# One more Strassen pair in the input projection of a hybrid layer, with bank pools in turn, other queue positions for right operands, and an approximate root with one Newton step

## The chip, the cores and the metric

The kernel runs on one core of a Trainium2 chip. The metric is device time in microseconds (us), of which the median of several runs is given. The engines are named as in the profile: PE (TensorE, matmuls; PEld its weight loads), DVE (VectorE), ACT (ScalarE), POOL (GpSimd), SP (SyncE, which issues the DMAs). SBUF is the memory of 128 partitions, PSUM holds eight banks of 128x512 float32 into which PE accumulates.

## The reference

One layer over 1024 positions of width 1024, in float32:

```python
u = rms_norm(x, norm1_g)
z = u @ w_in                      # 1024 x 3584: conv B, C, h; retention q, k, v, gate
y_conv = group_rms_norm(cb * causal_dwconv3(cc * ch, conv_w), conv_norm_g, 8)
q, k = rotary(rq), rotary(rk) * 128 ** -0.5
o = chunkwise_retention(q, k, v)  # 4 heads of 128, chunks of 128, per-head decay
y_ret = group_rms_norm(o, ret_norm_g, 4) * silu(rg)
x = x + concat(y_conv, y_ret) @ w_out
x = x + relu(rms_norm(x, norm2_g) @ w_up) ** 2 @ w_down
out = rms_norm(x, final_norm_g)
```

## The kernel before, in words

All data lies transposed: features on the partitions, the 1024 positions along the free axis in two halves of 512. So a matmul has a 128x128 block of weights as its left operand and 128x512 of data as its right, and sums into one bank. For accuracy each operand is split into a high part (`wh`, `uh`, `yh`, a cast on ACT) and the rest (`wl`, `ul`, `yl`, a subtraction on DVE or POOL), and each block product is three matmuls: high·high, high·rest, rest·high (`mm`, whose matmuls stand at line 375).

The input projection has 24 tiles f of 128 columns, plus v. A **whole** tile (`tile_in`) takes 8 blocks of rows and two halves of positions: 48 matmuls of 128x512. A **pair** of tiles (`pair_in`) is one Strassen-Winograd step over two column tiles, two halves of the rows and two halves of the positions: seven products, each over four blocks of 128 rows, 12 matmuls each. The left operands of the products are sums of weight blocks that `Left.split` makes on POOL; the right operands are quarters of x ("11", "21", "22") and four sums of them, t1 to t4. `rights(j)` makes these for the four row blocks j: it loads x again (`xs`), scales it on ACT, subtracts on DVE or POOL, casts the high part on ACT (`put_hi`, tile `U`) and subtracts for the rest (`put_lo`). Only t1, which product n=5 needs, is written over the second half of `uh[0..3]` and `ul[0..3]`, so it has to wait until the last whole tile has read these. The results of products are added into the two z tiles on DVE.

The order in time is: v; q and k of heads 0, 1 and then 2, 3 (whole tiles 12 to 19, with the retention as a background task that puts a few small matmuls between them); the whole tiles `IN_WHOLE[0]`, then the list `IN_WHOLE[1]`; the pairs `IN_PAIRS`; the output projection in four groups of two tiles; the MLP, also in Strassen products. Tiles 0 to 11 are the conv group (for conv block i, f = 3i is C, 3i+1 h, 3i+2 B), 12 to 19 retention's q and k, 20 to 23 its gates.

A tile's evacuation starts background tasks: `conv_h` (the product with h and the convolution of three taps), `conv_b` (the product with B, then the group norm) and `gate`. The norm of a conv block (`norm`) squares y on ACT, splits the squares, sums them over groups of 64 partitions with two matmuls against `blkr` (lines 455 and 456), takes the square root on ACT and the reciprocal on DVE, and multiplies y by it.

What stands where in each engine's queue is set by a planner at build time: `background` holds an estimated clock for each engine, with a cost per column (`Engine`), and `now` advances by `SLOT` per 12 matmuls. An operation is handed out when its estimated start is less than `LOOK` ahead of `now`, and, where it may go to DVE or POOL, to the one that would end first; matmuls of background tasks come when the task has been ready for `PE_MARGIN`. The queues themselves are served strictly in order. All operations of ACT, DVE and POOL go through the wrapper `Engine`, so that the profile has them at line 65; line 375 is `mm`, 554 to 621 the retention, 1195 the MLP's second product. Banks come from two pools of four, `pm` and `pr`.

Of the kernel before, what the change touches and what calls it, by code (L numbers as in the profile page):

```python
# [16 lines left out]
P = 128  # L17
# [17 lines left out]

IN_WHOLE = [[0, 1, 2], [3, 4, 5, 6, 7]]
IN_PAIRS = [(8, 9), (10, 11), (20, 21), (22, 23)]
IN_FIRST = [12, 13, 16, 17, 14, 15, 18, 19] + IN_WHOLE[0] + IN_WHOLE[1]  # L40
SLOT, LOOK, PE_MARGIN, LATE = 2.57, 2.0, 1.2, 0.0
UP_ORDER, MLP_ORDER = (1, 2, 5, 6, 3, 7, 4), (1, 2, 6, 5, 3, 7, 4)
IN_LAST = (1, 5, 2, 6, 7, 4, 3)


class Engine:


    def __init__(self, engine, per_column, now, clock):
        self.engine, self.per_column, self.now, self.clock = engine, per_column, now, clock  # L50
        clock[self] = 0.0

    def cost(self, n, op=""):
        return 1e-3 * n * (6.4 if op == "reciprocal" else self.per_column)

    def __getattr__(self, op):
        f = getattr(self.engine, op)

        def call(out, *args, **kw):
            n = 1  # L60
            for d in out.shape[1:]:
                n *= d
            begin = max(self.clock[self], self.now[0])
            self.clock[self] = begin + self.cost(n, op)
            return f(out, *args, **kw)  # L65

        return call
# [3 lines left out]
def hybrid_layer(  # L71
# [14 lines left out]
):  # L86
    nc = tc.nc
    now, clock, procs, got = [0.0], {}, [], {}
    act = Engine(nc.scalar, 1.02, now, clock)
    dve = Engine(nc.vector, 1.18, now, clock)  # L90
    pool = Engine(nc.gpsimd, 2.4, now, clock)
    gammas = [1.0 - 2.0 ** (-5.0 - h) for h in range(NH)]

    cp = ctx.enter_context(tc.tile_pool(name="cp", bufs=1))
# [81 lines left out]

    IN_ORDER = IN_FIRST + [f for pair in IN_PAIRS for f in pair]
    blocks = [w_in[f, c] for f in IN_ORDER for c in range(2)]
    blocks += [w_out[i, c] for j in range(4) for i in (j, 4 + j) for c in range(2)]
    mix = Stream(rw, blocks, 3)  # L180

    def next_piece():
# [4 lines left out]
    class Left:  # L187


        def __init__(self, stream, n_, order=UP_ORDER):  # L190
            self.stream, self.n = stream, n_
            self.five_first = 5 in order[:2]
            self.raw = None
# [36 lines left out]
    dve.memset(blk[64:128, 64:128], 1.0)  # L230
    blkr = xp.tile([P, P], F32R, name="blkr")
    dve.tensor_copy(blkr, blk)
    ident = cp.tile([P, P], F32, name="ident")
    make_identity(nc, ident)

# [164 lines left out]
    def background(look=LOOK):  # L400
        while True:
            best = None
            for task in list(procs):
                want = task.want
                if want is None:
                    if task.ready + PE_MARGIN <= now[0] or look > 1e6:
# [36 lines left out]
    def norm(y, w, inv_n, done):  # L443
# [11 lines left out]
        nc.tensor.matmul(b, w, sh, start=True, stop=False)  # L455
        nc.tensor.matmul(b, w, slo, start=False, stop=True)
        now[0] += 0.43
        parts_of_s[0] -= 1
# [6 lines left out]
        parts_of_s[0] -= 1  # L465

    def norms():
        while asked and parts_of_s[0] <= 2:
# [41 lines left out]
    def rot_tiles(ct, st):  # L510
# [21 lines left out]

        tile_in(evac)
        return q

    o_n, retention_task = {}, [None, None]

    def retention(p, q, k):
# [7 lines left out]
        for c in range(NC_ + 2):  # L546
# [28 lines left out]
            if done is not None:  # L575
# [83 lines left out]
    def conv_b(i, half, z, out, psum):  # L659
# [6 lines left out]
        eng.tensor_mul(o, o, cvs[i][:, sl])  # L666
        y[i] = out

        def done(rt):
# [42 lines left out]
    for p in range(2):  # L712
# [79 lines left out]
    def pair_in(fs, last):  # L792
# [3 lines left out]
        for at, n in enumerate(order):  # L796
            if not got.get("pairs") and n in (6, 7, 4):
                for j in range(4):
                    force(({6: "t2", 7: "t3", 4: "t4"}[n], j))
            b = product(n, pm)  # L800
            slot()
            prepare()
            ready = None
# [9 lines left out]
            if n == 6:  # L813
                dve.tensor_add(c12, acc, b5)
            if n == 7:
                dve.tensor_add(c22, acc, b5)
                ready = 1, 1
            if n == 3:
                dve.tensor_add(c12, c12, b)
                ready = 0, 1  # L820
            if n == 4:
                ready = 1, 0
# [622 lines left out]
```

## Time and profile before

| | |
|---|---|
| median of 3 runs | 1099.43 us (1099.06 to 1100.08) |
| the profiled execution, its time | 1098.8 us |
| its span in the trace | 1097.0 us |
| mean granted clock of PE | 0.986 of full speed |
| retention's last matmuls end | 208.4 us from the span's start |
| first matmul of the output projection | 366.49 us |

The stages up to 208 us are v, q, k and most of the retention with the whole tiles around it; 208 to 366 us hold the rest of the whole tiles and the four pairs; the output projection lasts to some 470 us, the MLP to the end. In the views a group shows the operation, "out<-in", its shape and count, then busy time and the mean of one; a wait shows the engine and line that waited and what released it.

### The profile page before, as it was taken

What the parts mean: (1) busy time and instruction counts of PE and PEld (TensorE: products, weight loads), DVE (VectorE), ACT (ScalarE), POOL (GpSimd) and SP (SyncE); (2) the same over time, 40 slices, a digit from 0 to 9 for tenths busy, and PEclk for the clock granted to TensorE, in tenths of its full rate; (3) what the DMA queues carried; (4) which work ended last, traced back from release to release, by engine and by line L of the source; (5) the groups of instructions that cost most, each with busy time, mean ns of one, the idle gap of its engine ahead of it and who ended that gap; (6) DMA issues with size and microseconds to landing.
All of it is one profiled execution on the core that took longest, in us unless ns stands there. A gap on an engine that the chain in (4) does not pass through costs nothing.

```text
span 1097.0 us, 13933 instructions
## 1 busy us (share of the span) xinstructions
PE 1064.2 (97%) x4916; PEld 885.6 (81%) x4916; DVE 874.1 (80%) x1206; ACT 461.6 (42%) x909; POOL 544.7 (50%) x377
## 2 busy tenths in 40 slices
PE   8999999998999899989999999999999999999997
PEld 6888888886777688878888888888888888888886
DVE  8446534597999756589999989989999899899945
ACT  8211344663435444435343433443443443334453
POOL 6133312264667213537729538358267185384553
PEclk9999999999999899989999999999999999999998
DMA  7111110510111525040130121211201301200204
GB/s 269 61 58 48 30 39 30 183 39 20 49 58 49 191 97 189 3 164 20 48 97 27 46 82 39 70 47 48 87 29 50 96 20 48 87 20 20 76 3 154
DMA packets 38869, 76.49 MB, mean 70 GB/s; under 512 B 4368, under 2 KB 6544, under 8 KB 38800
## 3 DMA queue, kind: packets, MB, share of 16 engines
q1 hardware_dynamic: 38800, 75.61, 21.2%
q8 instruction: 39, 0.64, 0.2%
q14 instruction: 30, 0.25, 0.1%
HBM read 68.78 MB, written 6.82 MB: 69 GB/s over the span
## 4 chain that ended last, share of the span: by engine, by line
PE 84%; DVE 10%; ACT 3%; issue 2%; POOL 1%; DMA 0%; SPq 0%; DVEq 0%; POOLq 0%; ACTq 0%
PE b L375 54%; PE b L1195 24%; PE b L331 2%; DVE wl L65 2%; DVE U L65 1%; DVE z L65 1%; ACT uh L65 1%; ACT t L65 1%; DVE cv L65 1%; DVE r L65 1%; DVE t L65 1%; PE b L583 1%; PE b L554 1%; DVE q L65 1%; PE b L312 1%
## 5 line engine op out<-in xcount | busy, mean ns | idle before, releaser
L65 ACT CAST wh<-r 128x512 fp32r<-128x512 f32 x286 | 177.2, 621 | 373.4 <-PE b L375 183.9
L65 DVE TENSOR_TENSOR wl<-r,wh 128x512 fp32r<-128x512 f32 x253 | 230.0, 912 | 106.5 <-ACT wh L65 105.8
L375 PE MATMUL b<-U,wh 128*128 128x512 f32 x992 | 308.1, 392 | 2.9 <-DVE U L65 2.9
L65 POOL TENSOR_TENSOR r<-r,r 128x512 f32<-128x512 f32 x136 | 208.2, 1533 | 126.5 <-DVE wl L65 77.5
L1195 PE MATMUL b<-V,wh 128*128 128x512 f32 x784 | 242.0, 389 | 0.4 <-POOL V L65 0.4
L375 PEld LDWEIGHTS b<-U,wh 128*128 128x128 f32 x992 | 187.5, 189 | 42.6 <-DVE U L65 3.4
L65 DVE TENSOR_TENSOR x<-x,b 128x512 f32<-128x512 f32 (+1 forms) x320 | 197.9, 663 | 26.5 <-PE b L375 25.8
L375 PE MATMUL b<-U,wl 128*128 128x512 f32 x496 | 194.2, 392 | 0.0
L1195 PEld LDWEIGHTS b<-V,wh 128*128 128x128 f32 x784 | 147.1, 188 | 31.8 <-POOL V L65 0.8
L65 POOL TENSOR_TENSOR t<-t,t 128x512 f32<-128x512 f32 x70 | 106.7, 1529 | 102.3 <-ACT t L65 56.0
L1195 PE MATMUL b<-V,wl 128*128 128x512 f32 x392 | 152.5, 389 | 0.0
L65 POOL TENSOR_TENSOR wl<-r,wh 128x512 fp32r<-128x512 f32 x33 | 44.2, 1341 | 150.7 <-ACT wh L65 126.2
L375 PE MATMUL b<-uh,wh 128*128 128x512 f32 x320 | 107.7, 401 | 4.0 <-DVE z L65 4.0
L375 PEld LDWEIGHTS b<-U,wl 128*128 128x128 f32 x496 | 93.8, 189 | 19.5
L375 PE MATMUL b<-ul,wh 128*128 128x512 f32 x320 | 106.0, 396 | 0.0
L375 PE MATMUL b<-uh,wl 128*128 128x512 f32 x320 | 105.6, 395 | 0.0
L1195 PEld LDWEIGHTS b<-V,wl 128*128 128x128 f32 x392 | 73.6, 188 | 15.2
L65 POOL TENSOR_TENSOR V<-t,V 128x512 fp32r<-128x512 f32 x35 | 48.7, 1393 | 68.4 <-ACT V L65 68.4
L65 DVE TENSOR_TENSOR t<-t,b 128x512 f32<-128x512 f32 x112 | 75.8, 677 | 1.7 <-POOL t L65 1.2
L375 PEld LDWEIGHTS b<-uh,wh 128*128 128x128 f32 x320 | 59.8, 192 | 16.4 <-issue 2.7
L375 PEld LDWEIGHTS b<-uh,wl 128*128 128x128 f32 x320 | 61.2, 191 | 13.3
L375 PEld LDWEIGHTS b<-ul,wh 128*128 128x128 f32 x320 | 60.9, 190 | 13.1
(158 smaller groups left out, 1424.7 us busy)
## 6 DMA issues: line engine op xcount, KB each, us to landing
r<-w_up_t SPq DMA_DIRECT2D x64, 256.0 KB, 2.6
r<-w_down_t SPq DMA_DIRECT2D x56, 256.0 KB, 2.6
r<-w_in_t SPq DMA_DIRECT2D x48, 256.0 KB, 2.6
xt<-xT SPq DMA_DIRECT2D x16, 256.0 KB, 5.4
xs<-xT SPq DMA_DIRECT2D x8, 512.0 KB, 7.3
r<-w_out_t SPq DMA_DIRECT2D x16, 256.0 KB, 2.6
x<-xT SPq DMA_DIRECT2D x8, 512.0 KB, 7.7
outT<-out SPq DMA_DIRECT2D x6, 512.0 KB, 2.9
```

What stands on the lines that cost most here:

```text
L65: return f(out, *args, **kw)
L312: nc.tensor.matmul(b[:, c * P : (c + 1) * P], d, ident, start=True, stop=True)
L331: nc.tensor.matmul(vb[i], a[k][:, tsl], b[k // 2][:, vs], start=(k == 0 and a is uh and b is vh), stop=(k == KT - 1 and a is ul),)
L375: nc.tensor.matmul(b, a[:, k, :], rhs(n, k)[r], start=(start and i == 0), stop=(stop and i == len(ops) - 1),)
L554: nc.tensor.matmul(bs[:, js[j]], k[j][:, sl], q[j][:, sl], start=True, stop=True)
L583: nc.tensor.matmul(bo[:, js[j]], sc[:, js[j]], vj[j], start=True, stop=(S is None))
L1195: nc.tensor.matmul(b, a, r, start=(i == 0), stop=(i == len(ops) - 1))
```

## The change

Tiles 6 and 7 leave the list of whole tiles and become the first of five pairs. The seven products of a pair take their banks from `pm` and `pr` in turn, and the last pair's order puts n=5 sixth, whose bank is then added to both z tiles where it was held until n=6 and n=7. `spread_norms` and the first three whole tiles come after the tasks `rights` are created, so that their queue positions can lie among conv and retention. The norm takes ACT's approximate reciprocal root `r`, and a square of it scaled by half the group's factor; DVE then multiplies that by the bank's sum (plus eps), which gives half of (mean + eps)·r², multiplies y by r and −g, and by (that − 1.5): one Newton step, y·g·r·(1.5 − ½(mean + eps)·r²). The retention's root on 128x2 gets a Newton step in the same way. `NORM_MARGIN` is the time that a norm's squares must have been ready before its matmuls are placed. The planner's costs become a fixed part and a part per column, with more for a DVE operation without a bank beside a busy POOL. In the output projection, the four steps of a group change their order, and with them the order of the weight blocks.

```diff
-IN_WHOLE = [[0, 1, 2], [3, 4, 5, 6, 7]]
-IN_PAIRS = [(8, 9), (10, 11), (20, 21), (22, 23)]
+IN_WHOLE = [[0, 1, 2], [3, 4, 5]]
+IN_PAIRS = [(6, 7), (8, 9), (10, 11), (20, 21), (22, 23)]
...
-SLOT, LOOK, PE_MARGIN, LATE = 2.57, 2.0, 1.2, 0.0
+SLOT, LOOK, PE_MARGIN, LATE = 2.72, 2.0, 1.2, 0.0
+NORM_MARGIN = 4.0
...
-IN_LAST = (1, 5, 2, 6, 7, 4, 3)
+IN_LAST = (1, 2, 6, 7, 4, 5, 3)
...
-    def cost(self, n, op=""):
-        return 1e-3 * n * (6.4 if op == "reciprocal" else self.per_column)
+    def cost(self, n, op="", bank=False):
+        per_column = 6.3 if op == "reciprocal" else self.per_column
+        cost = self.fixed + 1e-3 * n * per_column
+        if self.beside and not bank and op != "reciprocal":
+            begin = max(self.clock[self], self.now[0])
+            cost += min(cost, max(0.0, 0.6 * (self.clock[self.beside] - begin)))
+        return cost
...
-    act = Engine(nc.scalar, 1.02, now, clock)
-    dve = Engine(nc.vector, 1.18, now, clock)
-    pool = Engine(nc.gpsimd, 2.4, now, clock)
+    act = Engine(nc.scalar, 0.13, 0.95, now, clock)
+    pool = Engine(nc.gpsimd, 0.2, 2.5, now, clock)
+    dve = Engine(nc.vector, 0.13, 1.04, now, clock, pool)
...
-    blocks += [w_out[i, c] for j in range(4) for i in (j, 4 + j) for c in range(2)]
+    blocks += [w_out[i, c] for j in range(4) for c in range(2) for i in (j, 4 + j)]
...
-            part = split_piece({1: a11, 2: a12, 3: a12, 4: a22, 5: a21, 6: a11, 7: a21}[n])
+            s3 = a11 if self.seven_first else a21
+            part = split_piece({1: a11, 2: a12, 3: a12, 4: a22, 5: a21, 6: a11, 7: s3}[n])
...
-            if n == (2 if self.five_first else 5):
-                pool.tensor_sub(a21, a22, a11)
+            if n == (6 if self.seven_first else 2 if self.five_first else 5):
+                pool.tensor_sub(s3, a22, a11)
...
-        yield None
+        yield NORM_MARGIN
...
-        act.activation(rt, b, AF.Sqrt, bias=eps, scale=inv_n)
+        less = xp.tile([P, H], F32, tag="s", name=nm("r"), bufs=4)
+        act.activation(rt, b, AF.Abs_reciprocal_sqrt, bias=eps, scale=inv_n)
+        act.activation(less, rt, AF.Square, scale=(0.5 * inv_n) ** 0.5)
         yield (dve,)
-        dve.reciprocal(rt, rt)
-        yield from done(rt)
...
+        dve.scalar_tensor_tensor(less, b, EPS / inv_n, less, ALU.add, ALU.mult)
+        yield from done(rt, less)
...
-            dve.scalar_tensor_tensor(o, o, sm[:, CG + i : CG + i + 1], rt, ALU.mult, ALU.mult)
+            dve.scalar_tensor_tensor(o, o, less_g[:, i : i + 1], rt, ALU.mult, ALU.mult)
+            dve.scalar_tensor_tensor(o, less, 1.5, o, ALU.subtract, ALU.mult)
...
-                act.activation(m, m, AF.Sqrt)
-                dve.reciprocal(m, m)
+                m = rsqrt(m, xp.tile([P, 2, 2], F32, tag="m2", name=nm("m"), bufs=4))
...
-    spread_norms(rows_)
-    for f in IN_WHOLE[0]:
-        whole(f)
-
...
+    spread_norms(rows_)
+    for f in IN_WHOLE[0]:
+        whole(f)
     for f in IN_WHOLE[1]:
...
-            b = product(n, pm)
+            b = product(n, (pm, pr)[at % 2])
...
-            if n == 5:
-                b5 = b
...
+            if last:
+                if n == 6:
+                    act.copy(c12, acc)
+                if n == 7:
+                    act.copy(c22, acc)
+                if n == 5:
+                    dve.tensor_add(c22, c22, b)
+                    dve.tensor_add(c12, c12, b)
+                    ready = 1, 1
+            else:
+                if n == 5:
+                    b5 = b
+                if n == 6:
+                    dve.tensor_add(c12, acc, b5)
+                if n == 7:
+                    dve.tensor_add(c22, acc, b5)
+                    ready = 1, 1
...
-        steps = [(a, 0, 0), (a, 1, 0), (b, 0, 0), (b, 1, 0), (a, 0, 1), (b, 0, 1), (a, 1, 1), (b, 1, 1)]
+        steps = [(a, 0, 0), (b, 0, 0), (a, 1, 0), (b, 1, 0), (a, 0, 1), (b, 0, 1), (a, 1, 1), (b, 1, 1)]
```

Three places show what the planner makes of it. A row has the line, the operation, what is written, what is read, and the shape; the numbers behind the names tell tiles apart.

The first is ACT's queue ahead of the four casts `uh<-xs` of t1, on which product n=5 of the first pair rests. Before, where the last whole tiles run:

```order
L65 COPY a_2273<-b_2193 128x512
L65 COPY a_2273<-b_2194 128x512
L65 ACTIVATE r_2280<-b_2276,eps 128x512
L65 CAST wh_2309<-r_2180 128x512
L65 CAST wh_2339<-r_2077 128x512
L65 ACTIVATE cv_2348<-a_2273,sm 128x512
L65 CAST uh_142<-xs_1895 128x512
L65 CAST uh_143<-xs_1913 128x512
L65 CAST uh_144<-xs_1917 128x512
L65 CAST uh_145<-xs_1921 128x512
L65 CAST wh_2374<-r_2130 128x512
L65 COPY z_2360<-b_2361 128x512
```

After, from the last scaling of x for these transforms:

```order
L73 ACTIVATE xs_2120<-xs_2120,sm 128x1024
L73 CAST U_2220<-xs_2112 128x512
L73 CAST U_2227<-xs_2116 128x512
L73 CAST U_2231<-xs_2115 128x512
L73 CAST U_2235<-xs_2116 128x512
L73 CAST U_2238<-xs_2120 128x512
L73 CAST U_2242<-xs_2119 128x512
L73 CAST U_2245<-xs_2120 128x512
L73 CAST uh_144<-xs_1365 128x512
L73 CAST uh_145<-xs_2111 128x512
L73 CAST uh_146<-xs_2115 128x512
L73 CAST uh_147<-xs_2119 128x512
```

Before, the casts of t1 stand among weight casts (`wh`) and conv work of the whole tiles, far behind the casts of `U`; now they stand directly behind the last scaling, the casts of `U` for t2 to t4, and nothing else.

DVE's queue at the same place after the change, from the end of the last whole tile (its banks `b_2124` and `b_2125` are read by the first two rows) on, is next:

```order
L73 TENSOR_TENSOR z_2206<-b_2124,R 128x512
L73 TENSOR_TENSOR z_2206<-b_2125,R 128x512
L73 TENSOR_TENSOR U_2209<-xs_2112,U_2209 128x512
L73 TENSOR_TENSOR z_2206<-z_2206,cv_2138 128x512
L73 TENSOR_TENSOR U_2214<-xs_2111,U_2214 128x512
L73 TENSOR_TENSOR z_2206<-z_2206,cv_2138 128x512
```

```order
L73 TENSOR_TENSOR U_2235<-xs_2116,U_2235 128x512
L73 TENSOR_TENSOR U_2238<-xs_2120,U_2238 128x512
L73 TENSOR_TENSOR U_2242<-xs_2119,U_2242 128x512
L73 TENSOR_TENSOR U_2245<-xs_2120,U_2245 128x512
L73 TENSOR_TENSOR ul_152<-xs_1365,uh_144 128x512
L73 TENSOR_TENSOR ul_153<-xs_2111,uh_145 128x512
L73 TENSOR_TENSOR ul_154<-xs_2115,uh_146 128x512
L73 TENSOR_TENSOR ul_155<-xs_2119,uh_147 128x512
L73 TENSOR_TENSOR z_2256<-z_2257,b_2282 128x512
```

Between these two pieces stand eight rows of the same kinds: the `U` of the other parts and the differences `xs`. The four rows `ul` are the rest parts of t1, and the row behind them is the first addition of a product into z.

The second place is the norm on DVE, among the pairs. Before, at a gate's tile (`z_2690`) and the norm of conv block 2's y (`z_2528`):

```order
L65 TENSOR_TENSOR z_2689<-z_2690,b_2744 128x512
L65 RECIPROCAL r_2793<-r_2793 128x512
L65 TENSOR_TENSOR z_2689<-z_2689,b_2798 128x512
L65 TENSOR_TENSOR z_2690<-z_2690,b_2816 128x512
L65 TENSOR_TENSOR z_2690<-z_2690,b_2744 128x512
L65 SCALAR_TENSOR_TENSOR z_2528<-z_2528,sm,r_2793 128x512
L65 RECIPROCAL r_2795<-r_2795 128x512
L65 TENSOR_TENSOR wl_2854<-r_2684,wh_2853 128x512
L65 TENSOR_TENSOR z_2690<-z_2690,b_2840 128x512
L65 SCALAR_TENSOR_TENSOR z_2528<-z_2528,sm,r_2795 128x512
```

After, at a gate's tile (`z_2936`, `z_2937`) and the norm of the last conv block's first half (`z_2577`):

```order
L73 SCALAR_TENSOR_TENSOR o_834<-z_2751,sm,o_834 128x512
L73 SCALAR_TENSOR_TENSOR r_2932<-b_2928,r_2932 128x512
L73 TENSOR_TENSOR wl_2978<-r_2795,wh_2977 128x512
L73 TENSOR_TENSOR z_2936<-z_2937,b_2964 128x512
L73 SCALAR_TENSOR_TENSOR z_2577<-z_2577,less_g,r_2931 128x512
L73 SCALAR_TENSOR_TENSOR z_2577<-r_2932,z_2577 128x512
L73 TENSOR_TENSOR z_2937<-z_2937,b_2992 128x512
```

The reciprocal and the product with g are gone from between the additions of banks; a product with the bank `b_2928` and two products without a bank stand in their place.

The third is the end of the pairs on DVE, up to the splits of y. Before:

```order
L65 SCALAR_TENSOR_TENSOR o_1398<-z_2861,sm,o_1398 128x512
L65 TENSOR_TENSOR wl_3044<-r_2927,wh_3043 128x512
L65 TENSOR_TENSOR z_2860<-z_2860,b_3028 128x512
L65 SCALAR_TENSOR_TENSOR o_1398<-z_2861,sm,o_1398 128x512
L65 TENSOR_TENSOR z_2860<-z_2860,R 128x512
L65 TENSOR_TENSOR yl_3051<-o_1398,yh_3050 128x512
L65 SCALAR_TENSOR_TENSOR o_1397<-z_2860,sm,o_1397 128x512
L65 TENSOR_TENSOR yl_2931<-z_1875,yh_2930 128x512
L65 TENSOR_TENSOR yl_2935<-z_2186,yh_2934 128x512
```

After:

```order
L73 TENSOR_TENSOR wl_3097<-r_2955,wh_3096 128x512
L73 TENSOR_TENSOR z_2937<-z_2937,b_3081 128x512
L73 TENSOR_TENSOR z_2936<-z_2936,b_3081 128x512
L73 TENSOR_TENSOR wl_3121<-r_3009,wh_3120 128x512
L73 TENSOR_TENSOR z_2936<-z_2936,b_3105 128x512
L73 SCALAR_TENSOR_TENSOR z_2577<-z_2577,less_g,r_3044 128x512
L73 SCALAR_TENSOR_TENSOR z_2577<-r_3045,z_2577 128x512
L73 SCALAR_TENSOR_TENSOR o_1363<-z_2936,sm,o_1363 128x512
L73 TENSOR_TENSOR yl_3131<-z_2577,yh_3130 128x512
```

Before, the last addition of a bank (`z_2860<-z_2860,b_3028`) stood behind a product with o, a split of y and a weight split; now three additions, two of one bank, stand among weight splits, and the norm's last two products, the gates and the splits follow them.

More of the change, by code (lines that the diff above doesn't have):

```diff
@@ L34, with __init__ @@
 NSMALL = 44
-IN_WHOLE = [[0, 1, 2], [3, 4, 5, 6, 7]]
-IN_PAIRS = [(8, 9), (10, 11), (20, 21), (22, 23)]
+IN_WHOLE = [[0, 1, 2], [3, 4, 5]]
+IN_PAIRS = [(6, 7), (8, 9), (10, 11), (20, 21), (22, 23)]
 IN_FIRST = [12, 13, 16, 17, 14, 15, 18, 19] + IN_WHOLE[0] + IN_WHOLE[1]
-SLOT, LOOK, PE_MARGIN, LATE = 2.57, 2.0, 1.2, 0.0
+SLOT, LOOK, PE_MARGIN, LATE = 2.72, 2.0, 1.2, 0.0
+NORM_MARGIN = 4.0
 UP_ORDER, MLP_ORDER = (1, 2, 5, 6, 3, 7, 4), (1, 2, 6, 5, 3, 7, 4)
-IN_LAST = (1, 5, 2, 6, 7, 4, 3)
+IN_LAST = (1, 2, 6, 7, 4, 5, 3)
 class Engine:
-    def __init__(self, engine, per_column, now, clock):
-        self.engine, self.per_column, self.now, self.clock = engine, per_column, now, clock
+    def __init__(self, engine, fixed, per_column, now, clock, beside=None):
+        self.engine, self.fixed, self.per_column = engine, fixed, per_column
+        self.now, self.clock, self.beside = now, clock, beside
         clock[self] = 0.0
-    def cost(self, n, op=""):
-        return 1e-3 * n * (6.4 if op == "reciprocal" else self.per_column)
+    def cost(self, n, op="", bank=False):
[5 more added lines that the diff above has]
+        return cost
     def __getattr__(self, op):
@@ L62, in call @@
                 n *= d
+            bank = any(getattr(a, "space", None) == PSUM for a in args)
             begin = max(self.clock[self], self.now[0])
-            self.clock[self] = begin + self.cost(n, op)
+            self.clock[self] = begin + self.cost(n, op, bank)
             return f(out, *args, **kw)
@@ L192, in __init__ @@
             self.five_first = 5 in order[:2]
+            self.seven_first = order.index(7) < order.index(5)
             self.raw = None
@@ L232, in hybrid_layer @@
     dve.tensor_copy(blkr, blk)
+    less_g = cp.tile([P, 4], F32, name="less_g")
+    dve.tensor_scalar_mul(less_g, sm[:, CG : CG + 4], -1.0)
     ident = cp.tile([P, P], F32, name="ident")
@@ L404, in background @@
                 want = task.want
-                if want is None:
-                    if task.ready + PE_MARGIN <= now[0] or look > 1e6:
+                if want is None or isinstance(want, float):
+                    if task.ready + (want or PE_MARGIN) <= now[0] or look > 1e6:
                         best = (-1.0, task, None)
@@ L534, in rot_tiles, with rsqrt @@
         return q
+    def rsqrt(m, places):
+        r, t = places[:, 0], places[:, 1]
+        act.activation(r, m, AF.Abs_reciprocal_sqrt)
+        dve.tensor_mul(t, r, r)
+        dve.scalar_tensor_tensor(t, t, -0.5, m, ALU.mult, ALU.mult)
+        dve.scalar_tensor_tensor(r, t, 1.5, r, ALU.add, ALU.mult)
+        return r
     o_n, retention_task = {}, [None, None]
@@ L667, in conv_b, with done @@
         y[i] = out
-        def done(rt):
+        def done(rt, less):
             yield (dve,)
-            dve.scalar_tensor_tensor(o, o, sm[:, CG + i : CG + i + 1], rt, ALU.mult, ALU.mult)
+            dve.scalar_tensor_tensor(o, o, less_g[:, i : i + 1], rt, ALU.mult, ALU.mult)
+            dve.scalar_tensor_tensor(o, less, 1.5, o, ALU.subtract, ALU.mult)
             mark(("y", i, half), dve)
@@ L808, in pair_in @@
                 ready = 0, 0
-            if n == 5:
-                b5 = b
             if n in (6, 7, 4):
                 dve.tensor_add(acc, acc, b)
[L813 to L817, printed above, removed]
+            if n == 4:
+                ready = 1, 0
+            if last:
[15 more added lines that the diff above has]
+                    ready = 1, 1
             if n == 3:
@@ L820, in pair_in @@
                 ready = 0, 1
-            if n == 4:
-                ready = 1, 0
             if ready:
```

3 lines of the change are left out of this document (1 added, 2 removed).

## The prediction

> **What bounds the kernel now.** I read the page first (busy times, chain), then the waits of PE, then the program by stages, then the timelines of the stages that wait.
>
> ```profile
> PE 1064.2 (97%) x4916; PEld 885.6 (81%) x4916; DVE 874.1 (80%) x1206; ACT 461.6 (42%) x909; POOL 544.7 (50%) x377
> PE 84%; DVE 10%; ACT 3%; issue 2%; POOL 1%; DMA 0%; SPq 0%; DVEq 0%; POOLq 0%; ACTq 0%
> 489.99 16.34 PE b L375 x72
> ```
>
> PE sets the time: 97% busy, 84% of the chain. The third row, from the chain in the MLP, prices a 128x512 matmul in a stream: 16.34/72 = 0.227 us, a product of 12 at 2.72. So time is to be had from fewer matmuls, or where PE waits or runs at a lower clock. Here are the waits of PE between 100 and 480 us (total, times, longest), then the stages from the end of retention to the first out-projection matmul, with retention ahead (window, then busy us of PE, PEld, DVE, ACT, POOL, granted clock, DMA share):
>
> ```profile
> PE b L375 <- DVE z L65: 9.0, 3, 5.1
> PE b L455 <- ACT s L65: 4.0, 1, 4.0
> PE b L375 <- DVE U L65: 2.9, 1, 2.9
> PE b L583 <- ACT h L65: 1.8, 1, 1.8
> PE b L456 <- DVE s L65: 0.5, 2, 0.3
> ...
> 105.30:208.40 103.10, 101.10 (x602) 88.67 (x600) 51.18 (x124) 45.96 (x181) 25.57 (x19) 1.00 0.13 37
> 208.40:274.20 65.80, 61.55 (x266) 50.19 (x265) 53.64 (x49) 33.94 (x60) 34.51 (x23) 0.97 0.24 89
> 274.20:366.50 92.30, 82.96 (x346) 66.17 (x344) 89.07 (x90) 42.38 (x70) 59.88 (x40) 0.95 0.19 55
> ```
>
> In 274–366, the four Strassen pairs, DVE is busy 89.07 of 92.30 while PE idles 9.3: there **DVE is the bound**, and PE waits for its `z<-z,b` additions to free banks. At 257 PE waits 4.0 for the squares of a norm. After such a wait PE runs slow for some microseconds; the four places by clock:
>
> ```profile
> 257.40:262.00 4.60, 4.33 (x11) 3.25 (x12) 3.57 (x3) 2.25 (x4) 1.28 (x1) 0.63 0.00 0
> 319.00:323.00 4.00, 3.81 (x10) 3.03 (x11) 3.93 (x6) 0.24 (x1) 3.26 (x3) 0.57 0.00 0
> 356.50:361.00 4.50, 4.18 (x11) 3.32 (x12) 4.43 (x8) 0.38 (x1) 1.71 (x2) 0.62 0.39 117
> 366.40:371.00 4.60, 4.51 (x11) 3.62 (x12) 4.37 (x7) 3.30 (x6) 0.58 (x1) 0.54 0.91 281
> ```
>
> Lost in each is length × (1 − clock): 1.7, 1.7, 1.7 and 2.1, **7.2 us** in all. Waits and clock together make some 20 us between 208 and 371.
>
> The Trainium skill, "TensorE: Matmul & The Clock Gate", section "What's actually happening", says that the clock falls to half after an idle window of about 3.4 us. The trace differs: 2.0 and 1.9 us of waiting (319, 356) already cost a slow stretch, while the 1.8 us in retention left that stage at 1.00. By the page's rule two of the four losses, 3.4 us, would not be there to win and the sum below would be −3.7 instead of −7.1; the measurement decides.
>
> **The change part by part.** Pair (6, 7) replaces two tiles of 48 matmuls by seven products of 12: 96 → 84. At 0.227 each this is **−2.7**, and PE has no other new 128x512 work.
>
> The reciprocals on DVE go. The DVE groups from 208.4 to 366.5 (count, busy us, mean ns):
>
> ```profile
> L65 DVE RECIPROCAL r<-r 128x512 f32<-128x512 f32 x8 | 26.8, 3345 | 1.5 <-ACT r L65 1.5
> L65 DVE TENSOR_TENSOR wl<-r,wh 128x512 fp32r<-128x512 f32 x20 | 22.1, 1108 | 6.2 <-ACT wh L65 6.2
> L65 DVE TENSOR_TENSOR z<-z,b 128x512 f32<-128x512 f32 x28 | 18.8, 675 | 0.3
> L65 DVE TENSOR_TENSOR U<-xs,U 128x512 fp32r<-128x512 f32 x11 | 12.3, 1147 | 0.0
> L65 DVE SCALAR_TENSOR_TENSOR z<-z,sm,r 128x512 f32<-128x512 f32 x8 | 8.8, 1094 | 0.3
> ```
>
> A norm now costs one DVE operation with a bank (like `z<-z,b`, 0.68) and two without (0.75 to 1.10) where it cost 3.35 + 1.10: 4.45 → about 2.6, 15 us less over eight, and no piece longer than one pass. Against this stand seven more `z<-z,b` of the added pair, 4.7 us. ACT gets a square per norm (near the 0.69 of `r<-b`) and three table loads; with 42 of 92 us busy it hides them. The 128x2 replacements in retention are 0.16 to 0.2 us each and sit in a chain that waits once, 1.8 us: that wait I keep.
>
> Now DVE's sum for the pairs after the change. Its pace depends on POOL, as these rows at the end of the stage show:
>
> ```profile
> 357.92 0.68 DVE L65 TENSOR_TENSOR wl<-r,wh 128x512 fp32r<-128x512 f32 x1
> ...
> 360.00 1.73 POOL L65 TENSOR_TENSOR z<-z,R 128x512 f32<-128x512 f32 x1 [2.79 <-DVE z L65]
> 360.50 1.78 DVE L65 TENSOR_TENSOR wl<-r,wh 128x512 fp32r<-128x512 f32 x1
> 362.20 0.67 DVE L65 TENSOR_TENSOR z<-z,b 128x512 f32<-128x512 f32 x1
> ...
> 363.40 1.75 DVE L65 SCALAR_TENSOR_TENSOR o<-z,sm,o 128x512 f32<-128x512 f32 x1
> 365.07 0.68 DVE L65 TENSOR_TENSOR wl<-r,wh 128x512 fp32r<-128x512 f32 x1
> 365.67 0.67 DVE L65 TENSOR_TENSOR z<-z,b 128x512 f32<-128x512 f32 x1
> ...
> 366.49 0.77 PE L375 MATMUL b<-yh,wh 128*128 128x512 f32 x1 [5.09 <-DVE z L65]
> ```
>
> The same `wl<-r,wh` takes 0.68 alone and 1.78 beside POOL; the addition of a bank takes 0.67 either way. Starts lie about 0.08 closer than these durations, so a step is 0.60 and 1.70. From the late product below to the last one, PE has 396 matmuls, 89.8 us; DVE has 41 operations with a bank and 48 without: 41 × 0.60 + 48 × 0.60 + 1 for small ones = 54 us undisturbed. The 20 `wl` at a mean of 1.108 are 40% slow ones; with that share, 48 × 0.4 × 1.10 = 21 is added: **75 us against PE's 89.8**. So the waits of 2.0 and 1.9 in the pairs should go, and 4.0 + 0.5 at the norm, whose matmuls now stand behind more PE work. I leave 2.5 for what comes back; bounds are 0 and the 9.0 of before.
>
> At the end DVE's queue held 5.1 of wait. Now the last product is n=5, whose bank serves two additions at once; the bank that the first out-projection matmul needs is free some 0.75 after the last product, and the next splits come about 1.4 after it: **2.1 of wait, 1.7 of clock** (bounds: 0, and before's 5.1 + 2.1).
>
> The **new cost** is at the first pair. The six transforms of x for j = 1 to 3 stay behind the end of retention, but between it and product n=5, which needs t1, stood 284 matmuls (65 us of PE) and now stand 72 (one tile, 10.9; two products, 5.4) and small ones (0.6): PE is there 16.9 us after retention's end, T. ACT's and DVE's prices, from before's run of the same work:
>
> ```profile
> 218.77 3.23 ACT L65 ACTIVATE xs<-xs,sm 128x1024 f32<-128x1024 f32 x3
> 230.62 1.23 ACT L65 CAST U<-xs 128x512 fp32r<-128x512 f32 x2
> 235.30 2.39 DVE L65 TENSOR_TENSOR U<-xs,U 128x512 fp32r<-128x512 f32 x2
> 242.80 0.68 DVE L65 TENSOR_TENSOR xs<-xs,xs 128x512 f32<-128x512 f32 x1
> ...
> 205.54 4.27 SPq L753 DMA_DIRECT2D xs<-xT  x8
> ...
> xs<-xT SPq DMA_DIRECT2D x8, 512.0 KB, 7.3
> ```
>
> The last two rows are SP's: before, eight loads of x go out 2.9 us ahead of retention's end and land 7.3 after their issue in the middle. Now two of them stand among the weights of retention and six at the old place; they land by about T+4.4, ahead of ACT's first scaling, and the weights behind them (`r_2204` on) are not needed before the second pair.
>
> ACT does two heads' copies at T+5.5, four scalings at 1.04 each by T+10.7, then `wh_2200` when the tile ends at T+11.5, then two more scalings and thirteen casts at 0.53: 0.5 + 2.1 + 6.9, so T+21 if it never waits; the four casts of t1 are the last in that queue. The four `ul` behind them end at T+21.7 at best. DVE's two `z<-b,R` wait for the tile's end too, T+12.7; then come twenty operations without a bank: 12 us undisturbed, T+24.7; with the slow share of the eleven `U<-xs,U` of before, (1.147 − 0.68)/1.10 = 0.42, T+34. POOL has four operations in these 20 us (`wl_2201`, three on xs), each making one of DVE's slow, 4 × 1.1 at most: T+27 to T+29. I take T+27.5; the last three matmuls at the lower clock follow and the rest of the slow stretch, about T+29.6, where it would have been T+19.6. Behind ACT's casts stands `wh_2271` of the product after next, behind DVE's `ul` the first addition into `z`; both come before PE has done n=5 and the product after it: **+10** (bounds 4, from ACT's T+21.7, and 16.5, from T+34).
>
> Everything after the first out-projection matmul keeps its order but for the steps inside a group, which move evacuations by one step; the 2.9 behind `U` stays.
>
> Sum: −2.7 − 13.5 (9.0 + 4.0 + 0.5) − 7.2 + 10 + 2.5 + 2.1 + 1.7 = **−7.1**. The profiled execution took 1098.8 for a span of 1097.0; 1098.8 − 7.1 = 1091.7, and the median is 0.6 over the profiled one: **1092.3**.
>
> **The rivals.**
>
> t1 is not late: the scheduler's queues give way, for instance if xs land and scale ahead of the heads' copies. Against it: the order of ACT is fixed, and t1's casts stand behind nine casts of U. It takes back the 10: 1082.
>
> The waits come back elsewhere: with 4.7 us of additions more, DVE stays late in the pairs, which keep 3.9 of waits and 3.4 of clock where I count 2.5, and the end keeps its 5.1 + 2.1 where I count 3.8. −7.1 + 4.8 + 3.4 = +1.1: 1100.5, no change that can be measured. For it: 89 of 92 us were busy. Against it: the 75 above.
>
> **Slower:** DVE without a bank beside POOL. If the slow share in T+12.7 to t1 is s, its twenty operations end at T + 24.7 + 22s. My T+27.5 is s = 0.13. From s = 0.45 (T+34.6) the gain is gone, from 0.55 the loss can be measured; at 0.65 (T+39) the sum is −7.1 + 11.5 = +4.4, 1103.8, while the pairs (25.6 + 28.8 + 34.3 = 88.7) just fit under PE. For it: the 0.42 of the same operations in before is near, and five of them moved from POOL to DVE. Against it: POOL has little to do between `wl_2201` and the next `wl`, since that waits for a cast behind t1's.
>
> The Trainium skill, "SBUF — State Buffer", section "SBUF: two separate sides", states that a DVE operation with two SBUF inputs and a GpSimd operation exclude each other for a whole instruction. The 0.68 and 1.78 agree. By it the work of both adds up wherever they meet, which is this rival's mechanism and its 1103.8.
>
> **How the numbers follow.** Forecast (1086 to 1097) 0.58; t1 not late, 0.14; no gain, 0.14; slower, 0.12; 0.02 for anything else. A measurement of this kernel can tell about 0.2%, 2.2 us. The forecast's range and the first rival are below 1097.2: faster 0.73. The no-gain case straddles the mark: same 0.13, slower 0.14. The range goes from 1081 (t1 not late, a little better) to 1101 (no gain): it leaves out the slower case and tails.
>
> **What would show it.** Right: RECIPROCAL `r` gone from DVE's groups; a wait of PE for DVE `ul` or ACT `uh` of some 7 to 12 us near 251 (retention ends 112 matmuls, 25.4 us, later), with a slow stretch behind it; no wait of 2 us in the pairs; a first out-projection matmul near 360 instead of 366.5; DVE busy near 75 of the 90 us between. Wrong: no wait at t1 (first rival); PE at t1 more than 17 us late, with most of DVE's `U<-xs,U` near 1.8 (third); waits for `z` of 2 us or more in the pairs; or a difference after 506, where I predict none.

## The result and the profile after

| | before | after |
|---|---|---|
| median | 1099.69 us (4 runs) | 1105.28 us (4 runs, 1103.97 to 1105.97) |
| ratio of after to before | | 1.0052, 95% interval 1.004 to 1.0064 |
| span of the profiled execution | 1097.0 us | 1103.1 us |
| first matmul of the output projection | 366.49 | 372.66 |

The kernel became slower by 0.5%; the forecast was 1092.3, the range 1081 to 1101. Of the span's +6.1, all stands at the first matmul of the output projection (+6.2). Here are the page's busy times, and then the waits of PE from 90 to 490 us (total, times, longest), after the change:

```profile
PE 1057.8 (96%) x4904; PEld 881.8 (80%) x4904; DVE 871.1 (79%) x1246; ACT 471.5 (43%) x924; POOL 567.8 (51%) x392
```

```profile
PE b L387 <- DVE z L73: 14.9, 1, 14.9
PE b L387 <- ACT uh L73: 10.1, 1, 10.1
PE b L387 <- DVE U L73: 3.0, 1, 3.0
PE b L387 <- DVE wl L73: 1.1, 2, 0.9
PE b L387 <- DVE ul L73: 1.0, 1, 1.0
PE b L387 <- ACT wh L73: 0.4, 1, 0.4
```

The waits of before at the norm (4.0), in the pairs (2.0 and 1.9) and in retention (1.8) are gone, as is PE's work for 12 matmuls. Two waits took their place: 10.1 + 1.0 at product n=5 of the first pair, which the prediction had at 10 with the clock, and 14.9 for `z` at the end of the pairs, which it had at 2.1. Here is PE's row behind each of the two, and the first row of the product after n=5:

```profile
259.54 0.80 PE L387 MATMUL b<-uh,wh 128*128 128x512 f32 x1 [10.07 <-ACT uh L73]
...
265.57 0.62 PE L387 MATMUL b<-U,wh 128*128 128x512 f32 x2
...
372.66 0.76 PE L387 MATMUL b<-yh,wh 128*128 128x512 f32 x1 [14.86 <-DVE z L73]
```

The pairs by stages: from t1 on, the last six products, and the wait (window, busy us of PE, PEld, DVE, ACT, POOL, granted clock, DMA share):

```profile
262.00:340.00 78.00, 78.00 (x340) 64.45 (x339) 64.43 (x69) 32.07 (x53) 60.07 (x40) 0.98 0.18 51
340.00:357.80 17.80, 16.36 (x69) 12.26 (x67) 14.76 (x15) 12.13 (x20) 14.00 (x10) 1.00 0.21 60
357.80:372.66 14.86, 0.00 (x1) 0.03 (x1) 10.56 (x13) 9.40 (x15) 8.94 (x8) 0.59 0.19 53
```

PE runs through without a gap to 340, with eight banks in turn, and DVE falls behind it unseen: in the last row PE has nothing to do, while DVE is busy for 10.56 of 14.86 and ACT for 9.40. So neither is full; as the rows below show, they wait for each other. DVE's queue at that place (start, duration, and in brackets the idle time ahead and what ended it):

```profile
355.46 0.67 DVE L73 TENSOR_TENSOR z<-z,b 128x512 f32<-128x512 f32 x1
356.06 1.19 DVE L73 SCALAR_TENSOR_TENSOR o<-z,sm,o 128x512 f32<-128x512 f32 x1
358.38 1.77 DVE L73 TENSOR_TENSOR wl<-r,wh 128x512 fp32r<-128x512 f32 x1 [1.14 <-ACT wh L73]
360.08 0.68 DVE L73 TENSOR_TENSOR z<-z,b 128x512 f32<-128x512 f32 x1
360.68 1.81 DVE L73 SCALAR_TENSOR_TENSOR o<-z,sm,o 128x512 f32<-128x512 f32 x2
364.61 0.69 DVE L73 TENSOR_TENSOR wl<-r,wh 128x512 fp32r<-128x512 f32 x1 [2.12 <-ACT wh L73]
365.21 0.68 DVE L73 TENSOR_TENSOR z<-z,b 128x512 f32<-128x512 f32 x1
```

And ACT's:

```profile
356.17 0.62 ACT L73 COPY z<-z 128x512 f32<-128x512 f32 x1 [2.54 <-DVE z L73]
...
357.74 0.61 ACT L73 CAST wh<-r 128x512 fp32r<-128x512 f32 x1
360.79 0.62 ACT L73 COPY z<-z 128x512 f32<-128x512 f32 x1 [2.44 <-DVE z L73]
361.42 1.28 ACT L73 ACT_TABLE_LOAD   x1
362.72 0.69 ACT L73 ACTIVATE r<-b,eps 128x512 f32<-128x512 f32 x1
363.44 0.63 ACT L73 ACTIVATE r<-r 128x512 f32<-128x512 f32 x1
363.97 0.60 ACT L73 CAST wh<-r 128x512 fp32r<-128x512 f32 x1
364.59 1.28 ACT L73 ACT_TABLE_LOAD   x1
```

Read as one, this is a loop: DVE adds a product's bank to z (355.46); ACT's copy of c12 waits for that (356.17); the cast of the next weights stands behind the copy (357.74); DVE's weight split waits for the cast (358.38); and the next addition stands behind the split (360.08). A turn takes 360.08 − 355.46 = 4.62 and 365.21 − 360.08 = 5.13 us, where PE makes a product in 2.72. So at the end of the last product, 357.80, DVE has four of the last products to add still.

The loop is not all of it. DVE is late before the last pair begins: PE starts that pair at 335.84, and DVE adds the product before it, the last of the fourth pair, at 346.50. The last addition of all, of product n=3, is at 371.84, and the first matmul of the output projection follows its end.

```profile
335.84 0.39 PE L387 MATMUL b<-uh,wh 128*128 128x512 f32 x1
...
346.50 0.67 DVE L73 TENSOR_TENSOR z<-z,b 128x512 f32<-128x512 f32 x1
...
371.84 0.67 DVE L73 TENSOR_TENSOR z<-z,b 128x512 f32<-128x512 f32 x1
```

PE's last matmul of the fourth pair ended at 335.55, so DVE's lag was 10.9 us there. At the last product of all it was 14.0.

### The profile page after: what moved, and what is told of

The parts are those of the page before. It is cut to its first block, busy times and chain, and to the rows that moved or that the text cites. A ratio compares the mean times of both kernels' runs of the same rounds, so it can differ in the third digit from the quotient of the medians.

```text
span 1103.1 us, 13983 instructions
## 1 busy us (share of the span) xinstructions
PE 1057.8 (96%) x4904; PEld 881.8 (80%) x4904; DVE 871.1 (79%) x1246; ACT 471.5 (43%) x924; POOL 567.8 (51%) x392
## 4 chain that ended last, share of the span: by engine, by line
PE 84%; DVE 7%; issue 3%; POOL 3%; ACT 2%; DMA 0%; POOLq 0%; SPq 0%; DVEq 0%; ACTq 0%
PE b L387 52%; PE b L1228 23%; PE b L343 4%; DVE wl L73 2%; POOL z L73 1%; DVE z L73 1%; DVE cv L73 1%; POOL r L73 1%; DVE U L73 1%; DVE xs L73 1%; PE b L606 1%; PE b L577 1%; PE b L608 1%; PE b L614 1%; PE b L324 1%
## 5 line engine op out<-in xcount | busy, mean ns | idle before, releaser
L73 DVE TENSOR_TENSOR wl<-r,wh 128x512 fp32r<-128x512 f32 x255 | 240.0, 943 | 103.3 <-ACT wh L73 102.4
L387 PE MATMUL b<-U,wh 128*128 128x512 f32 x1016 | 314.7, 391 | 3.3 <-DVE U L73 3.0
L73 POOL TENSOR_TENSOR r<-r,r 128x512 f32<-128x512 f32 x140 | 214.3, 1533 | 119.9 <-DVE wl L73 71.6
L387 PEld LDWEIGHTS b<-U,wh 128*128 128x128 f32 x1016 | 191.1, 188 | 44.1 <-DVE U L73 3.4
L387 PE MATMUL b<-U,wl 128*128 128x512 f32 x508 | 198.4, 390 | 1.1 <-DVE wl L73 1.1
L387 PE MATMUL b<-uh,wh 128*128 128x512 f32 x304 | 102.9, 398 | 10.1 <-ACT uh L73 10.1
L387 PE MATMUL b<-ul,wh 128*128 128x512 f32 x304 | 101.3, 393 | 1.0 <-DVE ul L73 1.0
L387 PE MATMUL b<-uh,wl 128*128 128x512 f32 x304 | 100.9, 392 | 0.0
L1228 PEld LDWEIGHTS b<-V,wl 128*128 128x128 f32 x392 | 73.6, 188 | 15.1
L387 PEld LDWEIGHTS b<-uh,wh 128*128 128x128 f32 x304 | 56.2, 190 | 21.1 <-ACT uh L73 10.5
L73 ACT ACTIVATE t<-t 128x512 f32<-128x512 f32 x64 | 40.2, 631 | 74.6 <-DVE t L73 73.8
```

Source lines behind the costliest of these rows:

```text
L387: nc.tensor.matmul(b, a[:, k, :], rhs(n, k)[r], start=(start and i == 0), stop=(stop and i == len(ops) - 1),)
L1228: nc.tensor.matmul(b, a, r, start=(i == 0), stop=(i == len(ops) - 1))
```

## The experiments

**At the end of the pairs.** e1 and e2 set the loop against a plain lack of time on DVE, and test the banks. In e1 the additions go straight to their places:

```diff
-            if n in (6, 7, 4):
+            if n in (6, 7, 4) and not last:
                 dve.tensor_add(acc, acc, b)
...
                 if n == 6:
-                    act.copy(c12, acc)
+                    dve.tensor_add(c12, acc, b)
                 if n == 7:
-                    act.copy(c22, acc)
+                    dve.tensor_add(c22, c12, b)
+                if n == 4:
+                    dve.tensor_add(acc, c22, b)
```

> The last pair without its two copies on ACT: n=6 and n=7 add straight into c12 and c22, the same additions on DVE. Theory A (a loop at the end: addition on DVE, copy on ACT, weight cast behind it on ACT, weight split on DVE, next addition, some 4.5 us a turn against PE's 2.7): the wait of 14.9 us before the first out-projection matmul falls to 5 to 8, and the time by 7 to 9, to 1096 to 1098. Theory B (DVE has too much to do in the pairs, and eight banks instead of four only let PE run ahead and pay at the end): the wait stays above 12, the time at 1103 or more.

Measured: 1101.66 us, ratio 1.0023 (1.0013 to 1.0032); the last wait 11.1 instead of 14.9. Between the two theories: the copies are 3.7 of the wait, and 11.1 stands without them, about what DVE was late by before the last pair.

e2 takes all banks from one pool, `product(n, pm)`:

> All products from one pool of four banks; the order on every engine is that of the changed kernel. Theory A: PE waits among the last products instead of behind them, the sum of its waits for z stays near 15, time 1104 to 1107. Theory B: the same for the sum, but waits of 2 us show in the earlier pairs too. If alternation itself costs (another bank is waited for at the change of stage): the time falls by 3 or more.

Measured: 1105.11, ratio 1.0049 (1.0032 to 1.0067). Waits of 1.1 and 2.2 us for `z` come back at 320 and 337, and the last wait falls to 10.4; the first matmul of the output projection stands at 372.16 against 372.66. Alternation moves the waits to the end and wins nothing that can be measured.

**The late product n=5.** Retention's last chunk stands 112 matmuls later in the changed kernel than before. With the new costs each of retention's operations on 128 or 2 columns has a fixed part of 0.13 us or more in the planner, so that a chunk counts as ready later and is put further on; without that part the order has the chunk where it was. e3 drops it for small operations alone:

```diff
-        cost = self.fixed + 1e-3 * n * per_column
+        cost = (self.fixed if n > 2 * P else 0.0) + 1e-3 * n * per_column
```

> The planner's fixed cost only for operations of over 256 columns: retention's small operations cost what they cost before, and its last chunk is placed 112 matmuls earlier, as before. Theory C (t1 is late because retention ends late): the waits of 10.1 and 1.0 for uh and ul and the slow stretch behind them go, 11 to 13 us less, 1092 to 1094. Rival: the work on ACT and DVE that is then early meets DVE's queue in the pairs, the wait at the end grows by what is won, 1102 or more.

Measured: **1089.39**, ratio 0.9909 (0.9894 to 0.9924): 0.9% faster than before and some 16 us faster than the changed kernel. PE's waits at n=5 are 2.4 in three pieces, with no slow stretch behind them in this execution (granted clock 1.00 from 256 to 263; g1 below, with 2.2 in three pieces, has 0.51 there); and the last wait is 9.2, where the rival expected it to grow. Here are e3's waits of PE, and then its stages with the same cuts (t1 to the last products, these, the wait):

```profile
PE b L387 <- DVE z L73: 9.2, 1, 9.2
PE b L387 <- DVE U L73: 2.9, 1, 2.9
PE b L387 <- DVE ul L73: 2.4, 3, 1.0
PE b L643 <- ACT h L73: 2.1, 4, 0.8
```

```profile
258.00:330.00 72.00, 72.00 (x320) 59.58 (x319) 67.29 (x74) 30.38 (x49) 50.93 (x32) 1.00 0.16 50
330.00:348.50 18.50, 18.50 (x82) 15.01 (x80) 15.74 (x20) 13.79 (x23) 11.65 (x9) 1.00 0.20 58
348.50:357.75 9.25, 0.01 (x1) 0.03 (x1) 9.25 (x10) 3.23 (x7) 9.25 (x7) 0.77 0.32 86
```

In e3's last row DVE and POOL are both busy all of the 9.25: what is left of the wait is work, not the loop, and DVE was 7.8 late before the last pair (the table of lags stands under "The end" below). That is seen in e4, both edits together:

> Both edits. If A and C hold and are independent, 18 to 22 us less than the changed kernel: 1083 to 1087. If DVE's load is what remains (B), 1094 or more.

Measured: 1090.92, ratio 0.9926 (0.9909 to 0.9942), last wait 10.2. The copies cost nothing here. e3's last table load is at 338.50, and none stands between the last additions, where the changed kernel has two: ACT is ahead of DVE and no loop forms. The expectation that the two add up was wrong.

**The parts of the change, on top of e3.** f1 moves `less_g` behind the first splits, since in the profile after the first matmul stood at 6.05 instead of 5.25:

> On top of e3: the scaling that makes less_g stands behind the first splits of x and v instead of ahead of them. If it held DVE's first cast vh back until the small table had landed (first matmul at 6.05 instead of 5.25), the first matmul comes 0.5 to 0.8 earlier and the time is 1088.6 to 1088.9; if the cast waited for its own load anyway, 1089.4 and a first matmul near 5.8 to 6.

Measured: 1088.57, ratio 0.99 (0.9885 to 0.9915); the first matmul still at 6.05. In f2 to i2 it stood between 5.6 and 6.4 whatever was edited: PE waits there for DVE's first cast `vh`, and this for the landing of `wv`. So `less_g` has no effect on it. With one profile of before, it is not shown whether the change has a part in these 0.8 of the span's +6.1.

f2 has `IN_WHOLE` and `IN_PAIRS` of before:

> On top of e3: tiles 6 and 7 whole again, four pairs. If PE sets the time, 12 matmuls more, +2.7: 1092.1. If DVE sets it in the pairs, its lag at the end (9.2 us) is smaller with four pairs, by some 3 to 6 us, which gives 1086 to 1089.

Measured: 1093.15, ratio 0.9943 (0.9926 to 0.996), against 0.9909: the fifth pair wins about 3.7 us, the 2.7 of its matmuls and a shorter last wait (11.8 with four pairs), less the 2.4 of waits at n=5, which four pairs do not have. The rival, that it loads DVE, fell.

f3 has square root and reciprocal again in the norm:

> On top of e3: square root on ACT and reciprocal on DVE in the norm of 128x512, as before. DVE has about 2 us more for each of the norms in the pairs, and pieces of 3.35. If DVE's lag at the end is what is paid, the 9.2 us grow by 6 to 12: 1096 to 1101. If the lag comes from waits for ACT (table loads of the approximate root between silus), it falls, 1089 or less.

Measured: 1094.33, ratio 0.9948 (0.9934 to 0.9963): the Newton step wins some 4 us; with reciprocals the last wait is 12.6, and one of 1.8 comes back at a norm. The direction was right, the size two thirds of the lowest expected.

f4 records the additions ahead of `prepare()`:

> On top of e3: in a pair, the additions of a product are recorded ahead of the weight split that is prepared behind it. If the weight splits ahead of the additions in DVE's queue make the banks late at the end, the last wait falls by 2 to 4 and the time to 1085.5 to 1087.5; if DVE is simply full there, the weight splits are late instead, and the time stays within 1 of 1089.4 or grows.

Measured: 1091.22, ratio 0.9922 (0.9904 to 0.994); last wait 9.6. No gain: DVE is busy for 8.2 of these 9.6, and the wait now ends with a cast `yh` on ACT, which stands behind DVE's products with `o`.

g1 keeps the rest parts of y off POOL:

> On top of e3: the rest parts of y (yl) all on DVE, where POOL made six of them during the last products, at 1.7 us each beside DVE. If DVE's steps of 1.7 beside POOL make the last wait, each yl on DVE costs 0.6 and frees DVE's neighbours of 1.1: the wait falls by 1 to 4. If DVE's count of operations makes it, the wait grows by 2 to 4.

Measured: 1088.31, ratio 0.9892 (0.9873 to 0.9911). The last wait is 6.8, 2.4 less, but PE ends its products 2.6 later (351.16 against 348.51), and the output projection starts at 357.98 against 357.75. The 2.6 is not the edit's: PE is as late at the third pair already, behind a slow stretch at n=5 (granted clock 0.51 from 256 to 263, 1.00 in e3), and the profiled execution is the slowest of the four (1092.49). In the medians no difference can be told.

g2 has the steps and weight blocks of the output groups as before:

> On top of e3: the steps of an output group and their weight blocks in the order of before. The first three steps then need y of the gates one step (2.7 us) earlier. If those are late too, 1 to 3 us more; if the bank of the first matmul is all that is waited for, 1089 to 1090.

Measured: 1089.43, ratio 0.991 (0.9891 to 0.9929): no effect.

g3 is e2's edit on top of e3:

> On top of e3: all products from one pool of four banks. If alternation only moves PE's waits to the end (as e2 showed in the changed kernel), waits of some 2 us come back in the pairs, the last wait falls by as much, 1088.5 to 1091. If PE's run ahead is worth something here, 1092 or more.

Measured: 1090.37, ratio 0.9917 (0.9902 to 0.9933); one wait of 2.0 at 334 and a last one of 5.2. As e2: moved, not won.

**What makes the 14.9.** h1 leaves POOL's sums of weights out of the changed kernel, other engines' orders unchanged:

```diff
+    def sums(op, out, a, b):
+        if "mixer" in got:
+            op(out, a, b)
+        else:
+            clock[pool] = max(clock[pool], now[0]) + pool.cost(H)
...
-                pool.tensor_add(a21, a21, a22)
+                sums(pool.tensor_add, a21, a21, a22)
...
```

> The changed kernel without POOL's twenty sums of left operands in the pairs (each product then takes its weight block as loaded; this part of the computation is left out), every other engine's order as it was. If POOL's share of the common access, and the weight casts that wait for its sums, make DVE late, the last wait of 14.9 falls to 4 to 9 and the time by 6 to 11, to 1094 to 1099. If the loop through ACT (copies, table loads) and DVE's own count make it, the wait stays above 12 and the time above 1102.

Measured: 1097.14, ratio 0.997 (0.996 to 0.9981). The last wait is 11.1 and the one at n=5 7.9 instead of 10.1. The time was in the band, the wait between the theories: POOL's sums are 3.8 of it. From t1 to the output projection DVE is busy for 82.8 us (258 to 363) instead of 89.8 (262 to 372.66), with 96 instructions in both, while its weight splits wait no less for ACT's casts (15.1 instead of 13.9). So the sums cost by slowing DVE's operations beside them; that casts wait for sums is not seen to cost anything.

i1 has `AF.Copy` in place of `AF.Silu`; silu is left out, and no table load is left in the pairs:

> The changed kernel with a copy in place of silu in the gates (silu is left out), so that ACT loads no tables in the pairs; all orders as they were. Two table loads of 1.28 stand in the loop at the end and two ahead of it. If the loop through ACT makes the wait, it falls by 2.5 to 5, to 10 to 12.5; if DVE and POOL make it, by less than 1.

Measured: 1100.2, ratio 1.0009 (1.0 to 1.0019); last wait 11.95 instead of 14.86. The table loads are 2.9 of it.

i2 has the edits of e1, h1 and i1:

> The changed kernel without the two copies, without POOL's sums and without silu (sums and silu are left out). If the three add up: 14.9 - 3.8 - 3.8 - 2.6 to 4 = 3 to 5 of wait. If one hides behind another, 7 to 10.

Measured: 1094.26, ratio 0.9953 (0.9938 to 0.9968); last wait 8.2. The three overlap: they take 6.6 together, 3.7 + 3.8 + 2.9 = 10.4 apart. Its stages, cut as above:

```profile
259.00:335.00 76.00, 76.00 (x328) 62.65 (x328) 58.78 (x70) 33.04 (x55) 40.82 (x28) 0.97 0.17 53
335.00:353.00 18.00, 18.00 (x80) 14.60 (x78) 17.93 (x19) 10.92 (x19) 14.08 (x9) 1.00 0.26 74
353.00:361.30 8.30, 0.07 (x2) 0.08 (x1) 7.93 (x10) 2.29 (x4) 4.57 (x5) 0.64 0.26 64
```

Without the loop DVE is busy for 17.93 + 7.93 = 25.86 of the last 26.3 us, in which PE's work is 18. This remainder, some 8 us, is DVE's own work, with what POOL still slows of it; 5.4 of lag came from before the last pair.

i3 has all of the planner's costs of before:

> The changed kernel with all of the planner's costs of before (per column only, no term for a busy POOL). If the fixed part for small operations is all that hurt, 1088 to 1091 as in e3. If the term for DVE beside POOL helps, 2 to 6 more than e3; if it hurts, 2 to 6 less.

Measured: 1092.37, ratio 0.9935 (0.992 to 0.9949): better than the changed kernel by as much as e3 within some 3 us. The fixed part for small operations is nearly all of the harm; the rest of the new costs is worth about 0.26%, 2.8 us, with the intervals just meeting, so that even this is not certain.

## Why the prediction was wrong, point by point

**The late product n=5**: right in place and kind, priced too low. With T for retention's end, it was put at T+16.9 with a loss of 10; retention ended at 232.6 and PE stood from 249.47 (T+16.9) for 10.1 and 1.0 us, with a slow stretch behind. The product after n=5 started at 265.57, where 249.31 + 2.72 = 252.03 would have been possible: a loss of 13.5, inside the bounds of 4 and 16.5. How the stretch ran, DVE's groups from 249.4 to 262.5:

```profile
L73 DVE TENSOR_TENSOR U<-xs,U 128x512 fp32r<-128x512 f32 x9 | 5.9, 677 | 0.0
L73 DVE TENSOR_TENSOR ul<-xs,uh 128x512 fp32r<-128x512 f32 x4 | 2.5, 677 | 0.0
```

All of these at the undisturbed 0.68, as argued against the slower rival: the slow share in this stretch was not what made n=5 late. What the prediction missed is the start: DVE was through with the tile's `z<-b,R` at T+17.4 instead of T+12.7, behind the convolution and transforms `xs`, and t1 was ready at T+30.5 instead of T+27.5. Part of that is POOL after all: its sums held up the root of retention's last chunk (the rows in the last section) and the convolution's taps; in h1 the root's operations take 0.16 each, four taps 2.98 instead of 4.95, and the wait is 2.2 shorter. That the lateness was the planner's doing, and avoidable, the prediction did not see; e3 did.

**The pairs**: the waits of 2.0 and 1.9 went, as did the norm's 4.0. With one pool of banks, waits of 1.1 and 2.2 come back (e2), so the eight banks hid a lag of DVE. The sum behind that, DVE's 75 us against PE's 89.8, was too low: DVE had 54 operations without a bank instead of 48, and more of them slow (the `wl` below at a mean of 1.211 instead of 1.108). From 262 to 372.66 DVE was busy for 64.4 + 14.8 + 10.6 = 89.8 (by the three rows of the first section), and idle for 20.9, 13.9 of which in front of weight splits that waited for ACT:

```profile
L73 DVE TENSOR_TENSOR wl<-r,wh 128x512 fp32r<-128x512 f32 x25 | 30.3, 1211 | 14.2 <-ACT wh L73 13.9
```

**The end**: this is the step that failed. "The bank that the first out-projection matmul needs is free some 0.75 after the last product, and the next splits come about 1.4 after it: 2.1 of wait" took it for granted that DVE is level with PE at the last product, because its average load over the stage is below PE's. DVE was 10.9 us late already at the end of the fourth pair, and 9.5 at n=6 of the last (its last matmul ended at 345.94, DVE added it at 355.46). Eight banks let PE run on, so nothing showed of it until the end (e2, g3).

The next table has the lag from the end of a pair's last product on PE to the start of its addition on DVE, in us, found by counting products and additions in each trace.

| | pair 1 | pair 2 | pair 3 | pair 4 | last pair |
|---|---|---|---|---|---|
| after | 2.5 | 2.7 | 5.4 | 10.9 | 14.0 |
| e1, without the copies | 2.5 | 2.7 | 5.4 | 10.9 | 10.3 |
| h1, without POOL's sums | 1.1 | 1.1 | 3.6 | 5.5 | 10.3 |
| i2, without copies, sums and silu | 1.1 | 1.1 | 3.6 | 5.4 | 7.4 |
| e3, retention placed as before | 2.6 | 4.8 | 3.3 | 7.8 | 8.4 |

The lag grew in the third and fourth pair, and about half of the 10.9 goes with POOL's sums; in the last pair the loop with ACT adds some 3, which are gone without the copies. That pair also holds gates, the last norms, the splits of y and the splits of the next stage's weights beside its additions. The prediction also has n=5 as the last product; it is the sixth, and n=3 is the last. And "three table loads; with 42 of 92 us busy it hides them" counted ACT's busy share where the order counts: two of the loads and both copies stand in a loop with DVE. With 14.9 in place of the 2.1, the prediction's own sum is −7.1 + 12.8 = +5.7; the profiled execution was +6.1. That the two agree so well is in part luck: the 3.5 that n=5 cost beyond its 10 nearly cancels against retention's wait of 1.8, which the prediction kept and which went, and 1.0 of the 2.5 for what comes back (1.1 + 0.4 came).

**Product, Newton step, steps of the groups**: the −2.7 of the product held and was worth 3.7 on top of e3 (f2); fewer DVE operations in the norm were worth some 4 (f3); the order of the steps nothing (g2).

**The rivals**: "no gain" named the right quantity, DVE's lag at the end, with its 5.1 + 2.1 as the most that it could be; the slower case was given to another place, POOL's share ahead of t1. That share is 3.8 of the last wait (h1); at n=5 it cost 2.2, by way of what DVE does ahead of the twenty operations that the rival counts.

Not settled: why the fixed cost's order also lengthens the last wait, by 14.9 − 9.2 = 5.6 (from unrounded times). By the table of lags, 3.1 of that is there before the last pair (10.9 instead of 7.8), and the rest comes in it, where e3's order has no loop. Which differences in order make the 3.1 was not tried.

## What to carry to other kernels

An average load below the bound's says nothing of the end of a stage: walk the queue backwards from the hand-over and ask how far the helper engine lags there, and remember that more buffers only postpone the bill. When one engine's additions, another's copies and casts stand in each other's queues, price the turn of the loop, not the busy times. A planner's cost model is part of the kernel: a fixed 0.13 us on tiny operations moved the end of a background task by 25 us of matmuls and cost 16 (e3).

## What the runs showed of the hardware

DVE operations on 128x2, from SBUF, took 0.16 us alone, and up to 1.3 us beside POOL, where they ended with POOL's operation. This is the retention's root after the change, while POOL sums weights:

```profile
234.91 1.09 DVE L73 TENSOR_TENSOR m<-m 128x2 f32<-128x2 f32 x1 [0.27 <-ACT m L73]
236.04 0.16 DVE L73 SCALAR_TENSOR_TENSOR m<-m,m 128x2 f32<-128x2 f32 x1
236.24 1.14 DVE L73 SCALAR_TENSOR_TENSOR m<-m 128x2 f32<-128x2 f32 x1
```

POOL's timeline beside it:

```profile
233.33 4.03 POOL L73 TENSOR_TENSOR r<-r,r 128x512 f32<-128x512 f32 x3
```

The Trainium skill, "SBUF — State Buffer", section "SBUF: two separate sides", has the shared access held for a whole instruction; these rows agree, with 1.1 us paid for 2 columns: the last of them ends at 237.38, POOL's last sum at 237.36. Whether one reciprocal, as before, would be cheaper there is not shown: none of the 16 reciprocals of before stood beside POOL.
